# One more step of the main work between a modulation chunk's multiply-adds and its sums over partitions

## The chip, the cores and the metric

The kernel runs on one core of a Trainium2 chip. The metric is the device time of one execution in microseconds (us). Engines are named as the profile names them: PE (TensorE, the matrix engine; PEld is its weight load), DVE (VectorE), ACT (ScalarE), POOL (GpSimd) and SP (SyncE, which only issues DMA transfers here). PSUM is the small memory that PE writes; it is handed out in banks of 128 x 512 floats.

## The reference

Two layers work on x and ctx, each 256 tokens by 1024 (batch 1). Cut to what matters here:

```python
for l in range(2):
    mod_x = silu(c) @ w_mod[l] + b_mod[l]        # six vectors of 1024: shift, scale, gate, twice
    mod_c = silu(c_ctx) @ w_mod[l] + b_mod[l]    # the same weights, for ctx
    hx = rmsnorm(x) * (1 + sc1x) + sh1x;  hc = rmsnorm(ctx) * (1 + sc1c) + sh1c
    mx, mc = token_mixer(hx, hc, ...)             # half Fourier, half gated linear attention; w_in, w_out
    x = x + g1x * mx
    hx = rmsnorm(x) * (1 + sc2x) + sh2x
    x = x + g2x * channel_mixer(hx, l)            # layer 0: a dense FFN; layer 1: 8 experts, 2 per token
    if l == 0:
        ctx = ctx + g1c * mc;  hc = ...;  ctx = ctx + g2c * channel_mixer(hc, l)
return rmsnorm(x) * final_norm_w
```

All arithmetic is f32. A modulation is a matrix-vector product: one vector of 1024 against 1024 x 6144 weights, 24 MB a layer.

## The kernel before

**Main work.** Weights are streamed from HBM in units of 128 x 1024 floats, issued from SP's queue. Each unit is split into a high and a low part (ACT L148, DVE L152), and every product is three matmuls (L159, L160, L161). In time the program goes: mixer 0 (projections by w_in, attention, Fourier part, then w_out, whose results DVE scales and adds at L840 and L841), the FFN of layer 0 (three groups of an up phase, w1 and w3, and a down phase, w2, whose results DVE scales and adds at L1092 and L1093), mixer 1, then the experts. Each switch needs a norm: DVE scales a row block (L958), PE transposes it (L298), and ACT or DVE write the high and low parts of the blocks (low parts on DVE at L313), which are the operand of the next phase. The FFN's first up products take the blocks of ctx alone, half width, and then those of x.

**Modulations.** Of layer 0 the first two vectors are made at the start on PE. All the others, 20 chunks of 512 columns, are made beside the main work by `mod_chunk`, a Python generator. A chunk has four steps. Each loads a unit of w_mod (256 rows, 512 KB) into one of three places of a ring (`rr`, the first two tiles of it) and lets DVE multiply it by the entries of c and add it up in an accumulator of 128 x 512 (L422): one multiply-add for each 128 rows and each vector, so 4 a step where both x and ctx are wanted (`n_src` 2), else 2. Then the accumulator has to be summed over its 128 partitions: for a gate along rows by one matmul with a matrix of ones (L428) and a copy by ACT (L429), for shifts and scales along columns by four small matmuls (L432) and a copy by DVE (L434). The PSUM bank for it (`small`) comes from a ring of four that the main work uses as well.

**Order.** The main work advances the chunks by `pull(mods, 1)` after a step of its own: each pull runs the generator to its next `yield`. So the program's order on every engine is the order in which Python met the steps, but for priorities: the multiply-adds stand under `later(LATER)`, which lets a scheduler put them behind other work by a fixed amount, and splits are given high priority. Mixer 0 has 24 pulls and then takes what is left (`for _ in mods: pass`). It makes six chunks (the gate g of layer 0, 2; shift and scale for the FFN, 4; all for both vectors) and one step of constants. The FFN pulls twice for each of its 22 blocks of 128 and has further pulls in the down phases, 60 in all up to the third group's down phase, ahead of which it takes what is left (`while pull(m1, 1)`). It makes 14 chunks, the last two `gcol`, the second gate of layer 1.

**Gate weights of layer 1.** Behind that drain `gate_weights(1, ...)` loads 32 columns of w_in into the third place of the same ring, lets POOL spread them (L474), and ACT and DVE write their high and low parts (L478, L479) into `wl1`, which lies in the ring's first tile, where chunks load their weights too. Mixer 1 begins with products by `wl1`.

Of the kernel before, what the change touches and what calls it, by code (L numbers as in the profile page):

```python
# [74 lines left out]
def hybrid_kernel(ctx: ExitStack, tc: tile.TileContext, a: dict, out: bass.AP, dbg=None, upto="end"):  # L75
# [19 lines left out]
    def spot(i, n=1):  # L95
        return spots[i // 4][:, i % 4:i % 4 + n, :].rearrange("p a b -> p (a b)")
# [27 lines left out]
    def load_unit(src, shape, ring="raw", queue=None):  # L124
        n = shape[0] * shape[1]
        if ring == "mraw":
            raw = spot(2 * (turn["mraw"] % 3), 2)[:, :n]
            turn["mraw"] += 1
        else:
            raw = place_of("raw", n)  # L130
        ins = (queue or nc.sync).dma_start(raw.rearrange("p (a b) -> p a b", a=shape[0]), src).ins
        if queue:
            return raw, shape
        behind(ins, W.get("load"))
        W["unit"] = ins
        if chained():
            W["load"] = ins
        return raw, shape
# [16 lines left out]
    def wsrc(w2d, r0, nb, c0, cols):  # L155
        return w2d[r0:r0 + nb * 128, c0:c0 + cols].rearrange("(k p) c -> p k c", p=128)
# [83 lines left out]
    def small(shape):  # L240
        return ps0.tile([128, 512], F32, name="sc", tag="sc", bufs=4)
# [164 lines left out]
    def mod_chunk(l, col, n_src, rows_out=None, cols_out=None):  # L406


        accs = []
        for x in range(n_src):  # L410
            acc = spot(10 + x)
            nc.gpsimd.memset(acc, 0.0)
            nc.scalar.dma_start(acc[0:1, :], a["b_mod"][l:l + 1, col:col + 512])
            accs.append(acc)
        for q in range(4):
            raw, _ = load_unit(wsrc(a["w_mod"][l], q * 256, 2, col, 512), (2, 512), ring="mraw")
            rv = raw.rearrange("p (a b) -> p a b", a=2)
            for k in range(2):
                kb = q * 2 + k
                for x in range(n_src):  # L420
                    with later(LATER):
                        nc.vector.scalar_tensor_tensor(accs[x], rv[:, k, :], cs[:, x * 8 + kb:x * 8 + kb + 1],  # L422
                                                       accs[x], op0=OP.mult, op1=OP.add)
            yield
        for x in range(n_src):
            ps = small([128, 512])
            if rows_out is not None:
                nc.tensor.matmul(ps, ones, accs[x], start=True, stop=True)  # L428
                nc.scalar.activation(rows_out[x], ps, AF.Copy)  # L429
            else:  # L430
                for j in range(4):
                    nc.tensor.matmul(ps[:, j:j + 1], accs[x][:, j * 128:(j + 1) * 128], ones[:, 0:1],  # L432
                                     start=True, stop=True)
                nc.vector.tensor_copy(cols_out[x], ps[:, 0:4])  # L434
# [3 lines left out]
    def g_mod(l, which, n_src):  # L438
        col = (2 if which == 1 else 5) * D
        if (l, which) == (1, 2):  # L440

            for hh in range(2):
                yield from mod_chunk(l, col + hh * 512, n_src, cols_out=[gcol[:, hh * 4:(hh + 1) * 4]])
            return
        gp[l, which] = [hbp.tile([128, D], F32, name="g", tag="g1", bufs=1) if l else spot(6 + 2 * x, 2)
                        for x in range(n_src)]
        for hh in range(2):
            yield from mod_chunk(l, col + hh * 512, n_src,
                                 rows_out=[g[:, hh * 512:(hh + 1) * 512] for g in gp[l, which]])

    def s_mod(l, which, n_src):
        mc = modp.tile([128, 2, 16], F32, name="modc", tag="modc", bufs=2)
        modc[l, which] = mc
        for ch in range(4):
            yield from mod_chunk(l, (0 if which == 0 else 3) * D + ch * 512, n_src,
                                 cols_out=[mc[:, x, ch * 4:(ch + 1) * 4] for x in range(n_src)])
# [1410 lines left out]
```

## Time and profile before

| what | value |
|---|---|
| time, median of 3 runs | 1666.74 us (1665.79 to 1666.86) |
| time of the profiled execution | 1666.26 us |
| its span on the core | 1664.4 us |
| mean granted clock of PE | 0.989 of full speed |
| PE busy | 1603.6 us, 96% of the span |
| DVE busy | 1063.1 us, 64% |
| ACT busy | 724.5 us, 44% |
| multiply-adds of the chunks, L422 | 256 rows, 182.0 us |

The span is the stretch that the profiler sees on the core; 1.9 us lie around it. Busy shares are averages over stages that have different limits. The trace of one execution is read in stretches below: mixer 0 lasts to about 255 us, the FFN to 640 us, mixer 1 and the experts fill the rest.

### The profile page before, as it was taken

Reading aid. Unit: us, or ns where it says so; the run is one execution under the profiler, and the core shown is the slowest. Engines: PE = TensorE matmul, PEld = TensorE weight load, DVE = VectorE, ACT = ScalarE, POOL = GpSimd, SP = SyncE. Lnnn points to the kernel's source line nnn. Section 1 sums busy time; section 2 is a strip of 40 time slices with the busy share of each in tenths; the row PEclk is TensorE's granted clock in tenths of the full one; section 3 lists DMA queues with packets and bytes.
Section 4 is the critical chain, followed back from the end, with each engine's and each line's share of the span. In section 5 each row is a group of like instructions: output and inputs, shape, how many; then the busy total and the mean of one; then the engine's idle time right before and its main releaser. Section 6 shows DMA issues by size and latency. Waiting matters only on the chain.

```text
span 1664.4 us, 21388 instructions
## 1 busy us (share of the span) xinstructions
PE 1603.6 (96%) x8014; PEld 1148.3 (69%) x8014; DVE 1063.1 (64%) x1364; ACT 724.5 (44%) x886; POOL 27.5 (2%) x54
## 2 busy tenths in 40 slices
PE   6989999999999999999999989999999999999995
PEld 3867888788888888877787446874367843678431
DVE  3798897788567656865996226872458811688222
ACT  4733455322221247554784125752446710567111
POOL 1000000000000000000000000000000000000000
PEclk9999999999999999999999999999999999999997
DMA  9533385565655534555899999999999999999995
GB/s 372 160 104 126 101 269 154 163 190 169 198 190 191 167 124 134 174 165 215 306 337 322 417 415 414 408 416 417 414 414 413 402 384 415 413 412 411 407 409 202
DMA packets 172441, 479.05 MB, mean 288 GB/s; under 512 B 11777, under 2 KB 65153, under 8 KB 149537
## 3 DMA queue, kind: packets, MB, share of 16 engines
q1 hardware_dynamic: 170896, 473.80, 76.5%
q10 hardware_dynamic: 1074, 2.72, 0.5%
q8 instruction: 67, 1.10, 0.3%
q0 software_dynamic: 352, 1.00, 0.2%
q14 instruction: 52, 0.43, 0.1%
HBM read 476.43 MB, written 1.05 MB: 287 GB/s over the span
## 4 chain that ended last, share of the span: by engine, by line
PE 84%; DVE 6%; DMA 5%; ACT 3%; issue 1%; SPq 0%; POOL 0%; ACTq 0%; DVEq 0%; POOLq 0%
PE h L1647 12%; PE mm L159 8%; PE mm L160 8%; PE mm L161 8%; PE h L1656 6%; PE h L1659 6%; PE h L1655 6%; PE y L159 5%; PE y L160 5%; PE y L161 5%; PE y L1679 4%; DMA raw<-moe_w 3%; PE sc L601 1%; DVE lo L152 1%; PE sc L1624 1%
## 5 line engine op out<-in xcount | busy, mean ns | idle before, releaser
L180 DVE TENSOR_TENSOR rb<-raw,rb 128x2048 fp32r<-128x2048 f32 x72 | 164.8, 2291 | 174.7 <-ACT rb L180 160.3
L148 ACT ACTIVATE hi<-raw 128x1024 fp32r<-128x1024 f32 x127 | 134.5, 1059 | 303.1 <-PE mm L160 88.0
L152 DVE TENSOR_TENSOR lo<-raw,hi 128x1024 fp32r<-128x1024 f32 x127 | 155.2, 1223 | 80.9 <-ACT hi L148 79.5
L180 ACT ACTIVATE rb<-raw 128x2048 fp32r<-128x2048 f32 x72 | 138.1, 1918 | 119.2 <-DMA raw<-moe_w 62.8
L422 DVE SCALAR_TENSOR_TENSOR rr<-rr,cs,rr 128x512 f32<-128x512 f32 x256 | 182.0, 748 | 10.7 <-DMA rr<-b_mod 5.2
L1656 PE MATMUL h<-rb,hg 128*128 128x512 f32 x448 | 177.8, 397 | 4.0 <-DVE rb L180 4.0
L159 PE MATMUL mm<-hbk,hi 128*128 128x512 f32 (+1 forms) x456 | 166.5, 366 | 1.1 <-DVE tm L840 1.0
L160 PE MATMUL mm<-hbk,hi 128*128 128x512 f32 (+1 forms) x456 | 163.7, 360 | 0.5 <-DVE hbk L313 0.5
L161 PE MATMUL mm<-hbk,lo 128*128 128x512 f32 (+1 forms) x456 | 163.8, 359 | 0.0
L1647 PE MATMUL h<-raw,hgs 128*64 128x512 f32 (+1 forms) x608 | 134.3, 539 | 0.0
L1655 PE MATMUL h<-rb,hg 128*128 128x512 f32 x288 | 108.7, 399 | 5.1 <-ACT rb L180 5.1
L1656 PEld LDWEIGHTS h<-rb,hg 128*128 128x128 f32 x448 | 85.3, 190 | 26.9 <-DVE rb L180 6.8
L1647 PE MATMUL h<-rr,hgs 128*64 128x512 f32 (+1 forms) x416 | 98.2, 547 | 0.0
L159 PEld LDWEIGHTS mm<-hbk,hi 128*128 128x128 f32 x456 | 85.9, 189 | 16.6 <-issue 2.7
L160 PEld LDWEIGHTS mm<-hbk,hi 128*128 128x128 f32 x456 | 86.0, 189 | 14.1 <-issue 1.0
L161 PEld LDWEIGHTS mm<-hbk,lo 128*128 128x128 f32 x456 | 86.1, 189 | 13.1
L1647 PEld LDWEIGHTS h<-raw,hgs 128*64 128x64 f32 x608 | 45.5, 137 | 71.6 <-issue 66.6
L180 DVE TENSOR_TENSOR rb<-rr,rb 128x2048 fp32r<-128x2048 f32 x37 | 84.5, 2290 | 14.6 <-issue 8.5
L1659 PE MATMUL h<-rb,hg 128*128 128x512 f32 x288 | 89.0, 395 | 2.5 <-DVE hg L180 2.5
L160 PE MATMUL y<-rb,ht 128*128 128x512 f32 x224 | 88.8, 397 | 0.0
L180 ACT ACTIVATE rb<-rr 128x2048 fp32r<-128x2048 f32 x37 | 71.0, 1918 | 21.9 <-PE y L161 11.5
L1679 PE MATMUL y<-raw,hts 128*64 128x512 f32 x308 | 76.5, 601 | 3.5 <-DMA raw<-moe_w 3.4
(385 smaller groups left out, 2957.1 us busy)
## 6 DMA issues: line engine op xcount, KB each, us to landing
raw<-moe_w SPq DMA_DIRECT2D x180, 1024.0 KB
rr<-moe_w SPq DMA_DIRECT2D x106, 1024.0 KB
rr<-w_mod SPq DMA_DIRECT2D x80, 512.0 KB
raw<-ffn_w SPq DMA_DIRECT2D x72, 512.0 KB
raw<-moe_w SPq DMA_DIRECT2D x30, 768.0 KB
raw<-w_in SPq DMA_DIRECT2D x32, 512.0 KB
rr<-moe_w SPq DMA_DIRECT2D x18, 768.0 KB
raw<-w_out SPq DMA_DIRECT2D x23, 512.0 KB
```

The costliest lines, as they stand in the source:

```text
L148: ins = nc.scalar.activation(hi, raw, AF.Copy).ins
L152: nc.vector.tensor_tensor(lo, raw, hi.bitcast(F32), op=OP.subtract)
L159: nc.tensor.matmul(ps, lh, rh, start=start, stop=False)
L160: nc.tensor.matmul(ps, lh, rl, start=False, stop=False)
L161: nc.tensor.matmul(ps, ll, rh, start=False, stop=stop)
L180: r = getattr(self.engine, name)(*args, **kw)
L422: nc.vector.scalar_tensor_tensor(accs[x], rv[:, k, :], cs[:, x * 8 + kb:x * 8 + kb + 1], accs[x], op0=OP.mult, op1=OP.add)
L1647: nc.tensor.matmul(H[i][b][x * 64:x * 64 + 64, :n], HG[e][:, k0 + j, :], hi[:, j, o:o + n], start=(k0 + j == 0), stop=(k0 + j == 7))
L1655: nc.tensor.matmul(H[i][b], hgh[:, kb, :], hi[:, j, bc], start=(kb == 0), stop=False)
L1656: nc.tensor.matmul(H[i][b], hgh[:, kb, :], lo[:, j, bc], start=False, stop=False)
L1659: nc.tensor.matmul(H[i][b], hgl[:, kb, :], hi[:, j, bc], start=False, stop=(kb == 7))
L1679: nc.tensor.matmul(Y[e][0][hh * 64:hh * 64 + 64], ht[:, j0 + j, half], hi[:, j, xc], start=on, stop=off)
```

## The change

One `yield` is added between the four steps of a chunk and its sums. Nothing else differs; lines behind it move down by one (L428 becomes L429, L432 L433, L434 L435).

```diff
@@ mod_chunk
                         nc.vector.scalar_tensor_tensor(accs[x], rv[:, k, :], ...
                                                        accs[x], op0=OP.mult, op1=OP.add)
             yield
+        yield
         for x in range(n_src):
             ps = small([128, 512])
```

Before, the pull behind a chunk's fourth step made its sums and the next chunk's first step. Now that pull runs to the new `yield` and issues nothing; the sums and the next chunk's first step come one pull later. A chunk takes five pulls and not four: mixer 0's six chunks and one step of constants need 31 pulls and not 25, the FFN's 14 chunks 70 and not 56.

**The second chunk's sums (PE, in the attention of mixer 0).** L601 is the attention's score product, L159 to L161 are the projection by w_in, `rr_66` is the tile of the accumulators, `sqc` holds the ones. Before:

```order
L601 MATMUL sc<-ch_280,km 128x128 x8
L601 MATMUL sc<-ch_281,km 128x128 x8
L159 MATMUL mm<-rb_205,hi 128x512
L160 MATMUL mm<-rb_205,hi 128x512
L161 MATMUL mm<-rb_205,lo 128x512
L159 MATMUL mm<-rb_205,hi 128x512
L428 MATMUL sc<-rr_66,sqc 128x512 x2
L160 MATMUL mm<-rb_205,hi 128x512
```

After, one unit of w_in and a score product further on:

```order
L602 MATMUL sc<-ch_280,km 128x128 x8
L602 MATMUL sc<-ch_281,km 128x128 x8
L159 MATMUL mm<-hi,rb_205 128x512
L160 MATMUL mm<-lo,rb_205 128x512
L429 MATMUL sc<-rr_66,sqc 128x512 x2
L161 MATMUL mm<-hi,rb_205 128x512
```

The sums still stand just behind a score product, but two score products later than before; the first chunk's sums have moved one score product further.

**Between w_out of layer 0 and the FFN (DVE).** L840 and L841 (L841 and L842 after) scale and add the last results of w_out, L958 (L959) scales the two blocks of x for the norm, and L313 writes the low parts of x's blocks, with `h_2427` the first of them. Before:

```order
L264 TENSOR_TENSOR rsy<-rsy,rsv 128x1
L422 SCALAR_TENSOR_TENSOR rr_66<-rr_64,cs,rr_66 128x512
L958 TENSOR_SCALAR xn<-resid_1869,rsy 128x1024
L422 SCALAR_TENSOR_TENSOR rr_66<-rr_64,cs,rr_66 128x512
L422 SCALAR_TENSOR_TENSOR rr_66<-rr_65,cs,rr_66 128x512 x4
L313 TENSOR_TENSOR hbk<-h_2427,hbk 128x256
L313 TENSOR_TENSOR hbk<-h_2431,hbk 128x256
L309 TENSOR_SCALAR h_2440<-y,ac_2327,modc 128x256
L422 SCALAR_TENSOR_TENSOR rr_66<-rr_64,cs,rr_66 128x512
```

After:

```order
L422 SCALAR_TENSOR_TENSOR rr_66<-rr_64,cs,rr_66 128x512
L959 TENSOR_SCALAR xn<-resid_1869,rsy 128x1024
L422 SCALAR_TENSOR_TENSOR rr_66<-rr_64,cs,rr_66 128x512 x3
L422 SCALAR_TENSOR_TENSOR rr_66<-rr_65,cs,rr_66 128x512 x4
L422 SCALAR_TENSOR_TENSOR rr_66<-rr_64,cs,rr_66 128x512 x4
L313 TENSOR_TENSOR hbk<-h_2427,hbk 128x256
L313 TENSOR_TENSOR hbk<-h_2431,hbk 128x256
L309 TENSOR_SCALAR h_2440<-y,ac_2327,modc 128x256
```

From the last L840 pair to `h_2427` there are 10 multiply-adds in the order of before and 16 in that of after. From the last L584 of the attention, which stands about 70 us earlier, to that pair there are 34 and now 48. The 4 that stood among x's low parts have gone ahead of them. The last chunk's column sums (L432, now L433), which stood among w_out's products on PE with ctx's 16 transposes, now stand with the transposes behind the last of these products.

**Between w2 and mixer 1 (PE, then DVE).** L161 on `y` is the last product of w2, `rr_4850` holds the gate weights' parts. On PE, before:

```order
L161 MATMUL y<-hi,rb_4768 128x512
L159 MATMUL mm<-hbk,rr_4850 128x256
L160 MATMUL mm<-hbk,rr_4850 128x256
L161 MATMUL mm<-hbk,rr_4850 128x256
L159 MATMUL mm<-hbk,hi 128x256
```

After:

```order
L161 MATMUL y<-hi,rb_4719 128x512
L433 MATMUL mm<-sqc,rr_66 128x1 x4
L1076 MATMUL mm<-lgb,sqc 128x8
L298 MATMUL mm<-sqc,xn 128x128 x16
L159 MATMUL mm<-hbk,rr_4850 128x256
```

The last sum, the router's small matmul and the 16 transposes of ctx stood among the products of the up phase and of w2. On DVE, after, from the first half of the last results of w2 (L1093 and L1094 are L1092 and L1093 of before):

```order
L1093 TENSOR_TENSOR tm<-y,rr_65 128x512
L152 TENSOR_TENSOR lo<-raw,hi 128x1024
L422 SCALAR_TENSOR_TENSOR rr_66<-rr_65,cs,rr_66 128x512
L1094 TENSOR_TENSOR resid_1867<-resid_1867,tm 128x512
L422 SCALAR_TENSOR_TENSOR rr_66<-rr_64,cs,rr_66 128x512
L1093 TENSOR_TENSOR tm<-y,rr_65 128x512
...
L435 COPY gcol<-mm 128x4
L1077 COPY lgb<-mm 128x8
L263 TENSOR_SCALAR rsv<-rsv 128x1
L959 TENSOR_SCALAR rb_5243<-resid_1867,rsy 128x1024
L480 TENSOR_TENSOR rr_4850<-rr_67,rr_4850 128x512 x2
```

Where "..." stands, three more multiply-adds, one L1094 and six small steps of the norm follow. Before, all multiply-adds and L479 (now L480) stood in the up phase, and the low parts of ctx's blocks (L313) among the L1092 and L1093 of w2; now those low parts follow L480. On SP, the load of the 32 columns of w_in stands behind the last loads of w_mod, and these behind four of the first loads of mixer 1; before, it stood ahead of loads of w2.

## Rows read from the trace of the kernel before

**Rows 1.** The page: busy time of PE; shares of the chain that ended last.

```profile
PE 1603.6 (96%) x8014; PEld 1148.3 (69%) x8014; DVE 1063.1 (64%) x1364; ACT 724.5 (44%) x886; POOL 27.5 (2%) x54
PE 84%; DVE 6%; DMA 5%; ACT 3%; issue 1%; SPq 0%; POOL 0%; ACTq 0%; DVEq 0%; POOLq 0%
```

**Rows 2.** Windows: stretch, length, busy (and count) of each engine, clock, DMA, GB/s.

```profile
300.00:350.00 50.00, 50.00 (x227) 40.98 (x226) 38.08 (x52) 15.39 (x20) 2.10 (x4) 1.00 0.57 176
600.00:650.00 50.00, 49.17 (x258) 41.45 (x257) 36.72 (x68) 30.52 (x59) 0.00 (x0) 1.00 0.50 148
```

**Rows 3.** Waits of PEld, 20 to 640 us: total, times, longest.

```profile
PEld sc L428 <- issue: 4.9, 3, 3.8
PEld sc L428 <- PE mm L161: 1.0, 1, 1.0
```

**Rows 4.** Timeline of PEld at the second sums: start, length, instruction, [idle before].

```profile
120.44 0.19 PEld L159 LDWEIGHTS mm<-rb,hi 128*128 128x128 f32 x1
124.45 0.50 PEld L428 LDWEIGHTS sc<-rr,sqc 128*128 128x128 f32 x2 [3.83 <-issue]
...
127.17 0.32 PEld L160 LDWEIGHTS mm<-rb,hi 128*128 128x128 f32 x1 [0.52 <-issue]
```

**Rows 5.** Timeline of DVE over the same wait.

```profile
119.22 2.18 DVE L422 SCALAR_TENSOR_TENSOR rr<-rr,cs,rr 128x512 f32<-128x512 f32 x3
...
123.66 0.72 DVE L645 COPY_PREDICATED A<-masks,sc 128x512 f32<-128x512 uint8 x1
```

**Rows 6.** Window of 1 us behind that wait, columns as above.

```profile
125.00:126.00 1.00, 1.00 (x2) 0.34 (x1) 1.00 (x3) 0.00 (x0) 0.00 (x0) 0.50 0.85 303
```

**Rows 7.** Timeline of DVE from the attention to x's low parts.

```profile
185.94 8.03 DVE L422 SCALAR_TENSOR_TENSOR rr<-rr,cs,rr 128x512 f32<-128x512 f32 x12
...
264.41 3.40 DVE L422 SCALAR_TENSOR_TENSOR rr<-rr,cs,rr 128x512 f32<-128x512 f32 x5
267.72 0.77 DVE L313 TENSOR_TENSOR hbk<-h,hbk 128x256 fp32r<-128x256 f32 x2
```

**Rows 8.** Windows over that stretch, columns as in group 2.

```profile
186.00:208.00 22.00, 22.00 (x140) 18.00 (x140) 19.54 (x36) 9.42 (x20) 1.33 (x3) 1.00 0.25 73
208.00:255.60 47.60, 47.29 (x228) 38.97 (x226) 43.63 (x76) 26.15 (x47) 2.15 (x4) 1.00 0.80 255
255.60:273.70 18.10, 16.73 (x136) 16.32 (x137) 18.10 (x40) 10.09 (x24) 0.00 (x0) 1.00 0.53 152
```

**Rows 9.** Timeline of PEld, w_out's end and the first up product.

```profile
243.87 1.47 PEld L298 LDWEIGHTS sc<-sqc,xn 128*128 128x128 f32 x12
...
254.77 0.19 PEld L161 LDWEIGHTS mm<-hi,rb 128*128 128x128 f32 x1
256.38 0.19 PEld L159 LDWEIGHTS mm<-hbk,hi 128*128 128x128 f32 x1 [1.43 <-issue]
```

**Rows 10.** Timeline of PEld, the last sum and mixer 1's first product.

```profile
593.08 1.08 PEld L432 LDWEIGHTS mm<-sqc,rr 128*128 128x128 f32 x8
...
640.02 0.19 PEld L159 LDWEIGHTS mm<-hbk,rr 128*128 128x128 f32 x1
```

**Rows 11.** Timeline of DVE: gate weights, then the end of w2.

```profile
583.30 1.29 DVE L479 TENSOR_TENSOR rr<-rr,rr 128x512 fp32r<-128x512 f32 x2
...
640.63 1.28 DVE L1092 TENSOR_TENSOR tm<-y,rr 128x512 f32<-128x512 f32 x2
641.83 1.22 DVE L152 TENSOR_TENSOR lo<-raw,hi 128x1024 fp32r<-128x1024 f32 x1
642.97 1.29 DVE L1093 TENSOR_TENSOR resid<-resid,tm 128x512 f32<-128x512 f32 x2
```

**Rows 12.** Timeline of all engines: load and spreading of the gate weights.

```profile
576.06 0.37 SPq L131 DMA_DIRECT2D rr<-w_in  x1
...
579.88 2.07 POOL L474 COPY rr<-rr 128x128 f32<-128x128 f32 x4 [7.75 <-issue]
```

**Rows 13.** Waits of PEld, 640 to 665 us: total, times, longest.

```profile
PEld sc L298 <- DVE rb L958: 0.9, 1, 0.9
```

## The prediction

> **What bounds the kernel now.** I read the page first: PE is busy for 96% of the span and carries 84% of the chain that ended last [rows 1]. A change that neither adds nor removes PE work can gain only where PE waits and lose only where it makes PE wait. The windows say where that is. In the middle of the FFN PE is busy for 50.00 of 50 us, and DVE for 38.08 [rows 2]: a chunk's multiply-adds and sums have cover there, and moving them changes nothing. That leaves the places where PE idles in mixer 0, and the two joints at which the kernel takes what is left of the chunks at once, because the pulls no longer suffice: the end of mixer 0 and the end of the FFN's last up phase.
>
> **The first two sums.** The waits of PE's weight loads name L428 as the largest single line up to 640 us: 4.9 us in three waits, the longest 3.8, and 1.0 us once behind a product [rows 3]. At the second sums PE stands from 120.6 to 124.45 us [rows 4]. The multiply-adds they need ended at 119.22 + 2.18 = 121.4 us, but PE started only as DVE's first L645 was ending (123.66 + 0.72 = 124.38) [rows 5]. L645 reads the banks of the score product that stands just ahead, and the sums' banks come from the same ring of four. So of the 3.8 us I put some 1 us to the multiply-adds and the rest to the DVE queue and the bank. PE is then slow as well: the window from 125 to 126 us has a granted clock of 0.50 [rows 6], the 1.2 GHz level, and from 124.45 to about 127.8 us PE does 3.4 us of work that the full clock would do in 1.7. The two places thus hold 3.8 + 1.7 + 1.0 = 6.5 us.
>
> After the change the sums stand again a few products behind a score product, two scores later. The multiply-adds are long done by then, the bank is not. If each of the two sums keeps about 1.5 us of waiting for the bank and the clock stays up, 6.5 - 3.0 = 3.5 us are gained. The bounds are 0 (DVE is as late there) and 6.5.
>
> The clock by rows: one idle stretch of 3.83 us, then 0.50. The Trainium skill, page "TensorE: Matmul & The Clock Gate", section "Part 1: The HAM clock gate", says that an idle TensorE falls to its half clock and gets the full one back only with sustained work; the trace agrees here (0.50 behind 3.83 us). By that rule each new long wait of PE at the joints would cost a further 1.7 us (the price that the rows give for this one), and the sum below would be 3.4 us higher with both.
>
> **Joint 1, w_out to the FFN.** Here DVE sets the pace. From 255.6 to 273.7 us it is busy for all of 18.10 us, while PE has 1.4 us to spare [rows 8]; x's first low part starts at 267.72, straight behind five multiply-adds [rows 7], and PE needs it to go from ctx's half-width products to x's. By the order shown with the change, from the attention's last L584 to that low part DVE had 34 + 10 = 44 multiply-adds and has 48 + 16 = 64. Twelve in a row took 8.03 us, so 0.67 each [rows 7], and 20 more are 13.4 us. Against it stands the idle time of DVE in the same stretch: 22 - 19.54 = 2.46 us and 47.6 - 43.63 = 3.97 us [rows 8], 6.4 together, of which I take two thirds, 4.3, since the rest are waits for splits that more multiply-adds do not fill. And the stretch begins earlier by the 3.5 us gained above, which is where that gain is spent. 13.4 - 4.3 - 3.5 = 5.6 us later. The 4 multiply-adds that no longer stand among x's low parts give nothing back, since PE is paced by its own products behind the first block.
>
> PE's own side agrees in sign. The last chunk's column sums and 16 transposes (12 took 1.47 us [rows 9]) stand behind w_out's last product, so the gap of 254.77 to 256.38 us [rows 9] holds 1.1 us for each of two sums and 2.0 of transposes, and the ctx products start later, but they end in front of the same DVE wait. In the FFN behind it PE has no idle time in which to win the loss back [rows 2]. Bounds for the joint: 13.4 - 6.4 - 5 = 2 us (all idle time filled, and the first sums' full gain but for 1.5 us) and 13.4 - 3.5 = 9.9 us (none of it filled).
>
> **Joint 2, w2 to mixer 1.** Now the last product of w2 is followed without a gap by mixer 1's first product at 640.02 us [rows 10], because ctx's norm, its low parts and the gate weights were ready. After the change the last chunk and the gate weights stand behind w2. In the time of before:
>
> w2 ends earlier, since the transposes (2.0 us) and the last column sum (1.08 us [rows 10]) left it: 640.0 - 3.1 = 636.9 us. DVE takes 0.6 us to begin, as now (640.02 to 640.63 [rows 10, 11]), so at 637.5. Then four results at 0.6, one split at 1.14 (641.83 to 642.97 [rows 11]), five multiply-adds at 0.67 and 0.2 for small steps are 7.1 us: the last multiply-add ends at 644.6. PE's sum adds 1.1 us, and two transposes 0.25: 646.
>
> The gate weights take longer. Their load left SP at 576.06 us and POOL began at 579.88 [rows 12], 3.8 us later; from POOL's start to the end of L479 were 583.30 + 1.29 - 579.88 = 4.7 us [rows 11, 12]. In the new order the load is queued behind first loads of mixer 1, which wait for a raw buffer to be split; the last such split now lies between 639 and 641.5 us, so I take 640.5. Then 640.5 + 3.8 + 4.7 = 649.0 us. ctx's low parts stand behind L480 on DVE, so 0.4 us later PE starts: 649.5 us against 640.0, 9.5 us late. L480 cannot start before the last multiply-add either, since it goes into the ring's tile that these still read; that alone would give 644.6 + 1.15 (L478, taken as long as L479) + 1.3 + 0.4, some 647.5 us. During mixer 1's ctx products DVE finishes x's norm, so the 0.9 us that PE waits for it now [rows 13] go, and I add 0.8 us for the clock, half the price above. 9.5 - 0.9 + 0.8 = 9.4 us. Bounds: 647.5 - 640.0 - 0.9 = 6.6, less 1.6 us if some of the multiply-adds run while PE still works on w2, so 5; above, a load that leaves SP 2 us later and the full clock price, 13.
>
> The Trainium skill, same page, section "Architectural detail", says that VectorE's and ScalarE's queues are strictly first in, first out. That rule speaks against this change: L313 cannot pass L480. No run here shows it apart.
>
> **Sum.** Against the profiled execution, 1666.26 us (span 1664.4 and 1.9 around it, 0.5 under the median of the runs): 1666.3 + 5.6 + 9.4 = 1681.3. I say 1681 us.
>
> **The rivals.** Both joints late is the likeliest, 0.60, between 1666.3 + 2 + 5 = 1673 and 1666.3 + 9.9 + 13 = 1689.
>
> Only one joint costs, 0.19. For it speaks that each loss rests on a queue order, and DVE has free time in all stages; against it that DVE has none from 255.6 us on [rows 8] and that joint 2 puts a load, POOL, ACT and DVE in series behind the last product. Joint 1 alone gives 1672, joint 2 alone 1676.
>
> Both cost more, 0.08: both wake at the half clock, and the w_mod loads behind the first w_in loads come late, so that multiply-adds wait for data. That is 1689 and 2 to 5 us, 1692.
>
> Faster, 0.07: the sums' wait was for the multiply-adds after all, so that 6.5 us go; DVE then reaches joint 1 6.5 us early and fills its 6.4 us of idle time, which covers 12.9 of 13.4 us, and at joint 2 the DVE steps and the load run ahead while PE is still on w2. It decides from the point where joint 2 costs under 3 us. That gives 1660 to 1663.
>
> The change does nothing, 0.06: the sums wait for L645's bank as before, and the drained chunks run under other work. 1666.
>
> **How the numbers follow.** What a measurement of this kernel can tell from no change is about 0.2%, or 3.3 us. The forecast is the likeliest case. The range goes from 1671, which takes in either joint alone, to 1690, which takes in the upper bounds; outside lie no change and faster (0.13) and most of the heavy case. Faster 0.07, within 0.2% 0.06, slower 0.87.
>
> **What would show it.** Right: the waits for L429 fall from 5.9 us to about 3, with no window at 0.50 behind them; x's first low part comes some 5 us later than 267.7, behind a run of about 12 multiply-adds; PE has an idle stretch of 8 to 12 us between the last product on `y` and mixer 1's first, in which POOL's L474 and DVE's L480 run. Wrong: mixer 1's first product follows w2 within 3 us, or x's first low part is not later; or the experts' stage, which is not touched, gives back what the joints lost.

## The result, and the profile after

The changed kernel takes 1690.51 us (median of 5 runs, 1689.81 to 1695.15) against 1665.79 us before (median of 5 runs, two more than in the table above): slower by a factor of 1.0156, 95% interval 1.0144 to 1.0168. The factor is taken over all runs; the medians lie 24.7 us apart. The profiled execution has a span of 1688.7 us, 24.3 us more than before.

The page of the changed kernel, busy times and chain:

```profile
PE 1613.7 (96%) x8014; PEld 1158.6 (69%) x8014; DVE 1062.8 (63%) x1364; ACT 726.5 (43%) x886; POOL 27.1 (2%) x54
PE 83%; DMA 6%; DVE 5%; ACT 3%; issue 2%; SPq 1%; DVEq 0%; ACTq 0%
```

The work is the same (8014 matmuls, 1364 DVE instructions, as in [rows 1]). PE is busy 10 us longer, with the same matmuls: some of them ran at half the clock. The rest of the 24 us is idle time of PE. The waits of its weight loads, 20 to 700 us (total, times, longest; "issue" stands where the view names nothing that was waited for):

```profile
PEld mm L433 <- DVE rr L422: 8.6, 2, 8.3
PEld sc L433 <- issue: 5.9, 2, 5.7
PEld sc L429 <- issue: 4.6, 3, 2.5
PEld sc L429 <- PE sc L429: 0.4, 1, 0.4
PEld mm L159 <- ACT h L311: 4.2, 1, 4.2
```

The first row is the last sum of all, at the joint of w2 and mixer 1. The second is the last column sum of mixer 0, at the joint of w_out and the FFN. The third and fourth are the first two sums, 5.0 us together, which waited 5.9 us before [rows 3]. The last is mixer 1's first product.

**First joint.** The timeline of PEld, with the idle time ahead of an instruction in brackets:

```profile
249.63 0.19 PEld L161 LDWEIGHTS mm<-hi,rb 128*128 128x128 f32 x1
255.48 0.28 PEld L433 LDWEIGHTS sc<-sqc,rr 128*128 128x128 f32 x1 [5.66 <-issue]
```

DVE meanwhile, and up to x's first low part:

```profile
255.39 0.74 DVE L422 SCALAR_TENSOR_TENSOR rr<-rr,cs,rr 128x512 f32<-128x512 f32 x1
257.38 0.16 DVE L435 COPY modc<-sc 128x4 f32<-128x4 f32 x1 [1.25 <-PE sc L433]
...
259.09 0.16 DVE L435 COPY modc<-sc 128x4 f32<-128x4 f32 x1 [0.95 <-PE sc L433]
...
271.47 7.38 DVE L422 SCALAR_TENSOR_TENSOR rr<-rr,cs,rr 128x512 f32<-128x512 f32 x11
280.19 0.76 DVE L313 TENSOR_TENSOR hbk<-h,hbk 128x256 fp32r<-128x256 f32 x2 [1.34 <-ACT hbk L312]
```

PE has loaded the last weights of w_out at 249.8 us and soon stands, until DVE is at its last multiply-add of that chunk (255.39 + 0.74 = 256.1; the accumulators of x and ctx are done one after the other). Then DVE stands for PE's sum, and at the end for the block that ACT writes from PE's transposes. x's first low part comes at 280.19, 12.5 us after the 267.72 of [rows 7].

PE was slow in between as well. The transposes of x, which follow ctx's half-width products, began at 278.10 us, 16.0 us after the first of these products; before they began 8.6 us after it. The clock fell a second time there, behind a stretch in which PE was busy for 2.03 of 4 us (windows; columns as in [rows 2], where the engines stand in the order PE, PEld, DVE, ACT, POOL, and the clock is the third figure from the end):

```profile
264.00:268.00 4.00, 2.03 (x12) 1.41 (x11) 3.90 (x12) 3.95 (x11) 0.00 (x0) 0.92 0.01 2
268.00:272.00 4.00, 3.26 (x13) 2.79 (x14) 4.00 (x11) 1.66 (x5) 0.00 (x0) 0.50 0.41 131
```

DVE is busy all the same (3.90 and 4.00 us of 4). So, by the trace, the slow products show in x's first low part only by the 1.34 us that DVE waits at their end.

**Second joint.** PEld:

```profile
648.87 0.19 PEld L161 LDWEIGHTS y<-hi,rb 128*128 128x128 f32 x1
657.33 1.78 PEld L433 LDWEIGHTS mm<-sqc,rr 128*128 128x128 f32 x8 [8.27 <-DVE rr L422]
659.00 0.55 PEld L1076 LDWEIGHTS mm<-lgb,sqc 128*128 128x128 f32 x2
659.28 3.46 PEld L298 LDWEIGHTS mm<-sqc,xn 128*128 128x128 f32 x16
666.94 0.29 PEld L159 LDWEIGHTS mm<-hbk,rr 128*128 128x128 f32 x1 [4.19 <-ACT h L311]
```

The gate weights' last step on DVE, then the low parts of ctx's first two blocks; and on ACT the first and the last steps that read ctx's transposes:

```profile
660.48 1.28 DVE L480 TENSOR_TENSOR rr<-rr,rr 128x512 fp32r<-128x512 f32 x2
...
661.98 0.76 DVE L313 TENSOR_TENSOR hbk<-h,hbk 128x256 fp32r<-128x256 f32 x2
```

```profile
660.62 1.02 ACT L311 ACTIVATE h<-mm,modc,ac 128x256 f32<-128x256 f32 x2 [2.11 <-PE mm L298]
...
665.87 1.02 ACT L311 ACTIVATE h<-mm,modc,ac 128x256 f32<-128x256 f32 x2
```

Mixer 1's first product starts at 666.94 us and not at 640.02 [rows 10], 26.9 us late. The gate weights were ready at 661.76; the product waited 5.2 us longer. Its own block, the first, was ready as well (661.98 + 0.76 = 662.7 for two of them). The product started as ACT's last L311 ended (665.87 + 1.02 = 666.9), and L311 writes no block: it reads the transposes out of their bank of PSUM. So by the trace the product waited for a bank that still held transposes of ctx; no run tries that by itself. ACT's steps begin only when the transposes have come, and the transposes stand behind the sum on PE. Of the 26.9 us the stages behind give back 2.6 (the spans differ by 24.3), nearly all of it the experts' stage, which begins 26.7 us late; what did that was not tried.

The clock behind both idle stretches, in windows:

```profile
258.00:260.00 2.00, 2.00 (x10) 2.00 (x11) 1.05 (x5) 0.00 (x1) 0.52 (x1) 0.50 0.58 217
660.00:662.00 2.00, 2.00 (x11) 2.00 (x10) 1.85 (x5) 1.38 (x4) 0.00 (x0) 0.50 0.00 0
```

### The profile page after: what moved, and what is told of

It is laid out like the page before. It is cut to its first block, busy times and chain, and to the rows that moved or that the text cites. A ratio compares the mean times of both kernels' runs of the same rounds, so it can differ in the third digit from the quotient of the medians.

```text
span 1688.7 us, 21385 instructions
## 1 busy us (share of the span) xinstructions
PE 1613.7 (96%) x8014; PEld 1158.6 (69%) x8014; DVE 1062.8 (63%) x1364; ACT 726.5 (43%) x886; POOL 27.1 (2%) x54
## 4 chain that ended last, share of the span: by engine, by line
PE 83%; DMA 6%; DVE 5%; ACT 3%; issue 2%; SPq 1%; DVEq 0%; ACTq 0%
PE h L1648 11%; PE mm L159 9%; PE mm L160 8%; PE mm L161 8%; PE h L1657 6%; PE h L1660 6%; PE h L1656 6%; PE y L160 5%; PE y L159 5%; PE y L161 5%; PE y L1680 4%; DMA raw<-moe_w 4%; PE sc L602 1%; PE sc L1625 1%; DMA rb<-w_mod 1%
## 5 line engine op out<-in xcount | busy, mean ns | idle before, releaser
L148 ACT ACTIVATE hi<-raw 128x1024 fp32r<-128x1024 f32 x127 | 134.4, 1059 | 309.7 <-PE mm L160 88.2
L152 DVE TENSOR_TENSOR lo<-raw,hi 128x1024 fp32r<-128x1024 f32 x127 | 155.2, 1223 | 86.4 <-ACT hi L148 85.3
L422 DVE SCALAR_TENSOR_TENSOR rr<-rr,cs,rr 128x512 f32<-128x512 f32 x256 | 181.4, 746 | 4.1 <-DMA rr<-b_mod 1.6
L159 PE MATMUL mm<-hbk,hi 128*128 128x512 f32 (+1 forms) x456 | 167.6, 369 | 1.8 <-ACT hbk L312 1.7
L160 PE MATMUL mm<-hbk,hi 128*128 128x512 f32 (+1 forms) x456 | 166.1, 365 | 1.0 <-DVE rsv L263 0.9
L161 PE MATMUL mm<-hbk,lo 128*128 128x512 f32 (+1 forms) x456 | 165.1, 362 | 0.0
L159 PEld LDWEIGHTS mm<-hbk,hi 128*128 128x128 f32 x456 | 87.5, 192 | 17.2 <-ACT hbk L312 2.5
L161 PEld LDWEIGHTS mm<-hbk,lo 128*128 128x128 f32 x456 | 87.8, 193 | 12.9
L180 DVE TENSOR_TENSOR rb<-rr,rb 128x2048 fp32r<-128x2048 f32 x37 | 84.4, 2289 | 14.2 <-issue 9.1
L180 DVE TENSOR_TENSOR rb<-raw,part 128x2048 fp32r<-128x2048 f32 x32 | 73.2, 2289 | 10.6 <-ACT part L180 7.7
```

Source lines behind the costliest of these rows:

```text
L148: ins = nc.scalar.activation(hi, raw, AF.Copy).ins
L152: nc.vector.tensor_tensor(lo, raw, hi.bitcast(F32), op=OP.subtract)
L159: nc.tensor.matmul(ps, lh, rh, start=start, stop=False)
L160: nc.tensor.matmul(ps, lh, rl, start=False, stop=False)
L161: nc.tensor.matmul(ps, ll, rh, start=False, stop=stop)
L180: r = getattr(self.engine, name)(*args, **kw)
```

## The experiments

Two theories stood at first. A: the loss is the chunks that the pulls no longer reach; they are drained at the two joints with PE standing there. B: the step itself costs, in every chunk.

**The step in one of the two places alone.** A flag that `mods0` and `mods1` set, in the changed kernel:

```diff
             yield
-        yield
+        if more[0]:
+            yield
```

In mixer 0 alone:

> The added step stands only in the six chunks of mixer 0. Theory A (the loss is the last chunk that the pulls no longer reach, drained behind w_out and behind w2, with PE standing there): only the first joint costs, 1674 to 1678 us, first full-width product some 10 us late, and the w2 to mixer 1 joint without an idle stretch, as before. Rival B (every chunk loses because its accumulator is held one step longer): six of twenty chunks, 24.7 x 6/20 = 7 us, 1673, spread over mixer 0 and with no idle stretch of 5 us in front of L433. Rival C (the two joints add more together than alone): under 1670.

Measured: 1678.21 us, ratio 1.0069 (1.0051 to 1.0088), 0.2 us above A's range. In the FFN alone:

> The added step stands only in the FFN's 14 chunks. Theory A: only the joint of w2 and mixer 1 costs, 1680 to 1684 us, with PE idle some 8 us in front of L433 and again some 4 us in front of mixer 1's first product. Rival B: 14 of 20 chunks, 24.7 x 14/20 = 17 us, 1683, but lost over the up phases. Rival C: under 1676.

Measured: 1680.98 us, ratio 1.0092 (1.0072 to 1.0111). Against their before (1666.43) the two lose 11.8 and 14.6 us, 26.3 together, where both at once lost 24.7. So the joints add, which disposes of C. B's times lie too near to be told from A's, but the trace of the first run has 5.67 us of idle time in front of the last sum, where B had no stretch of 5.

**The same drains without the step.** The kernel of before with fewer pulls:

```diff
         for _ in tok(U0, tl, sink_u):
             pull(G, 1)
-            pull(mods, 1)
```

> The kernel of before, without the added step; the four pulls in the loop over U of mixer 0 are left out, so that as much of the last chunks is left for the drain as in the changed kernel. Theory A: the drain alone does it, so it costs what the changed kernel lost at the first joint plus the some 3.5 us that the first sums had gained: 1677 to 1682 us. Rival B: sums directly behind their multiply-adds cost nothing, 1665 to 1669.

Measured: 1678.28 us, ratio 1.0078 (1.0056 to 1.01). The other drain:

```diff
-            pull(m1, 2)
+            pull(m1, 2 if f < 10 else 1)
```

> The kernel of before, without the added step; the FFN pulls once and not twice for its blocks 10 to 21, so that the last two chunks are drained as in the changed kernel. Theory A: as with the added step in the FFN alone, 1680 to 1684 us, PE idle some 8 us in front of the last sum. Rival B: 1665 to 1669.

Measured: 1679.71 us, ratio 1.0086 (1.0065 to 1.0107), 0.3 us under A's range. Without any added step both lose what the step loses. PEld in the second of them:

```profile
637.74 0.19 PEld L161 LDWEIGHTS y<-hi,rb 128*128 128x128 f32 x1
646.20 0.93 PEld L432 LDWEIGHTS mm<-sqc,rr 128*128 128x128 f32 x4 [8.27 <-DVE rr L422]
```

It is the wait of the changed kernel, 8.27 us (8.1 in the run with the step in the FFN alone). B falls.

**The step with enough pulls.** If only the drains cost, more pulls should cure it. First in both places, the extra ones of mixer 0 in the loops over V and G:

```diff
             pull(G, 1)
-            pull(mods, 1)
+            pull(mods, 2)
...
-            pull(m1, 2)
+            pull(m1, 3 if f < 10 else 2)
```

> The added step, with pulls added so that none is missing: mixer 0 pulls twice in the loops over V and G (32 for 31), the FFN three times for its first ten blocks (70 for 70). The first sums then stand where they stood before. Theory A (the whole loss is the chunks that the pulls no longer reach): no idle stretch over 2 us at either joint, 1664 to 1668 us, as before. Rival B (the step itself costs): 1672 and above.

Measured: 1676.18 us, ratio 1.0061 (1.0046 to 1.0077). Then with those of mixer 0 in the loop over U and in the Fourier part:

> The added step, with the missing pulls added later in mixer 0 (twice in the loops over U and the Fourier part) and as in the run before in the FFN. The first sums stand where the changed kernel has them. Theory A: the gain at the first two sums (3.7 us earlier at the end of the attention in the changed kernel) stays and nothing is lost: 1661 to 1664 us, if the six chunks' multiply-adds, now crowded into the last third of mixer 0, do not make DVE late at w_out; 1665 to 1669 if they do. Rival B: 1672 and above.

Measured: 1675.72 us, ratio 1.0064 (1.0051 to 1.0078). A missed both, by 8 and by 7 us. The times are where B put them, but the trace doesn't show B's reason. The second joint is cured; in the run with late pulls PE is busy from 600 to 650 us:

```profile
600.00:650.00 50.00, 49.94 (x235) 41.23 (x234) 36.20 (x62) 29.03 (x51) 2.01 (x4) 1.00 0.49 145
```

The first joint is not, though no chunk is left for it. DVE there, in the same run:

```profile
266.99 6.71 DVE L422 SCALAR_TENSOR_TENSOR rr<-rr,cs,rr 128x512 f32<-128x512 f32 x10
273.61 0.76 DVE L313 TENSOR_TENSOR hbk<-h,hbk 128x256 fp32r<-128x256 f32 x2
```

x's first low part is 5.9 us later than in [rows 7], behind ten multiply-adds in a row where five stood. In the run with early pulls it is 8.8 us later. Nor is mixer 0 all of the loss: at mixer 1's first product the runs are 9.4 and 10.8 us late. In both PE waits 1.4 us for ACT's L148 and 0.9 us for DVE's L152 where the FFN first turns to w2 (at 350.25 and 351.93 us in the run with late pulls), which it did not before; the extra pulls stand in the blocks ahead of that turn. To settle the FFN by itself, the step there alone with three pulls from block 10 on:

> The added step in the FFN's 14 chunks alone, with pulls added (three instead of two from the FFN's block 10 on), so that nothing is left for the drain in front of w2's last phase. If the FFN's step costs only by the chunks that it leaves for that drain: as before, 1664 to 1668 us, no idle stretch over 1.5 us between 600 and 650 us. If the step itself costs in the up phases: 1670 and above.

Measured: 1666.46 us, ratio 0.9999 (0.999 to 1.0009). So in the FFN A holds: the 14.6 us come from the drain and, within 0.1%, none from the step, if the pulls stand in the later blocks.

**Mixer 0: who is short there?** Two runs on the kernel of before. One gives the first two sums the later place and pushes no multiply-add back. The sums of these two chunks are kept and made ahead of the next chunk's second load:

```diff
-            acc = spot(10 + x)
+            acc = rows_out[x] if wait else spot(10 + x)
...
+        owed.append(sums)
+        if not wait:
+            pay()
...
+            if q == 1:
+                pay()
             raw, _ = load_unit(wsrc(a["w_mod"][l], q * 256, 2, col, 512), ...
```

> The kernel of before, with the sums of its first two chunks alone made one step later, behind the next chunk's first step, so that no pull is spent and no multiply-add moves back (these two chunks add up in the tiles of their result rows, so that the next chunk does not need their accumulators). Theory A, sharpened: the step costs only by the multiply-adds that it pushes back, and gains at the first two sums, so this has the gain alone: the waits in front of these sums fall from 5.9 us to 2 to 4, no 0.50 window behind them, 1660 to 1664 us. Rival D: DVE is the limit of mixer 0 from the attention on, so that PE gets the 3 us early to the joint and waits there: 1665 to 1667.

Measured: 1666.5 us, ratio 1.0004 (0.9995 to 1.0013): no gain. The time is D's, but not for D's reason: the waits in front of these sums are still 5.6 us, and the clock still falls:

```profile
99.77 0.30 PEld L438 LDWEIGHTS sc<-rr,sqc 128*128 128x128 f32 x2 [2.51 <-issue]
```

```profile
100.00:104.00 4.00, 4.00 (x8) 1.93 (x8) 4.00 (x8) 1.75 (x4) 0.00 (x0) 0.57 0.30 111
```

DVE is busy for all 4.00 us there. The sum starts 0.07 us after DVE's first reading of the score product (98.98 + 0.72 = 99.70 us) has ended, as in [rows 4, 5]. The other run pulls chunks earlier, without the step:

```diff
         for _ in tok(U0, tl, sink_u):
             pull(G, 1)
-            pull(mods, 1)
+            pull(mods, 2)
```

> The kernel of before, without the added step, with two pulls for one in mixer 0's loop over U, so that its last two chunks come four pulls earlier and nothing is left to take at its end. If multiply-adds done before the joint are what counts there, x's first low part comes 2 to 5 us earlier: 1661 to 1664 us. If DVE is full in the Fourier part as well, PE waits there for the low parts of its own operands and it is no gain: 1665 to 1672.

Measured: 1671.86 us, ratio 1.0034 (1.0021 to 1.0047). The time lies in the second range, but PE does not wait for low parts. Now an earlier column sum waits for its multiply-adds (the first of two ends at about 154.5 us):

```profile
154.61 0.52 PEld L432 LDWEIGHTS sc<-sqc,rr 128*128 128x128 f32 x4 [3.18 <-issue]
```

Earlier costs, later costs: in each of the runs that moved pulls of mixer 0, PE stood for DVE somewhere.

**What holds PE at the joints.** In the changed kernel, half of the multiply-adds of the two drained last chunks left out:

```diff
-            for k in range(2):
+            for k in range(1 if half else 2):
```

> The changed kernel with half of the multiply-adds of the two drained last chunks left out (8 of 16 in mixer 0, 4 of 8 of gcol's second half; their results are then not the reference's), all loads, sums and orders left in. If DVE's multiply-adds in front of the drained sums hold PE: 8 x 0.67 = 5.4 us less at the first joint, whose wait in front of L433 all but goes, and 4 x 0.67 = 2.7 us less at the second, 1681 to 1684 us. Rival (the load of the last unit, or the order of the sum and the transposes on PE, holds it): within 2 us of the changed kernel, 1688 to 1691.

Measured: 1681.02 us, ratio 1.0096 (1.008 to 1.0111), 9.5 us less than the changed kernel. The last sum of the first joint waits 0.32 us and not 5.66, and x's first low part comes at 272.17 and not 280.19. That is 8.0 us earlier where the multiply-adds alone are 5.4: the rest is idle time of DVE, 6.1 us from the attention's last L584 to that low part, as before (6.4), and not 8.65. At the second joint:

```profile
646.48 0.71 PEld L433 LDWEIGHTS mm<-sqc,rr 128*128 128x128 f32 x3 [5.22 <-DVE rr L422]
```

5.22 us and not 8.27: less by 3.05, where 4 x 0.67 = 2.7 was worked out. So DVE's multiply-adds hold PE at both joints.

**The order of sum and transposes at the second joint.** The last sum taken out of the drain and made behind w2:

```diff
-            while pull(m1, 1):
-                pass
+            pull(m1, 10)
...
-                    pull(m1, 1)
+                    pull(m1, 0 if last else 1)
```

> The changed kernel with the very last sum (gcol's second half, wanted only behind the experts) left out of the drain and made behind w2, so that it no longer stands in front of ctx's 16 transposes; its multiply-adds and the gate weights stay where they are. Theory Q (PE stands at the sum while the transposes and so ctx's blocks are queued behind it): the transposes go back among w2's products, mixer 1's first product follows L480 and no longer ctx's blocks, 4 to 6 us less: 1684 to 1687 us. Rival (multiply-adds and gate weights alone hold mixer 1): within 1 us of the changed kernel, 1689.5 to 1691.

Measured: 1690.6 us, ratio 1.0155 (1.014 to 1.0171), no different from the changed kernel. Its trace shows why the gain was small and did not last:

```profile
650.55 0.19 PEld L161 LDWEIGHTS y<-hi,rb 128*128 128x128 f32 x1
661.51 1.78 PEld L433 LDWEIGHTS mm<-sqc,rr 128*128 128x128 f32 x8 [10.77 <-issue]
663.69 0.29 PEld L159 LDWEIGHTS mm<-hbk,rr 128*128 128x128 f32 x1 [0.40 <-issue]
```

```profile
659.16 1.45 POOL L475 COPY rr<-rr 128x128 f32<-128x128 f32 x4 [19.82 <-DMA rr<-w_in]
```

```profile
662.03 1.29 DVE L480 TENSOR_TENSOR rr<-rr,rr 128x512 fp32r<-128x512 f32 x2
```

Mixer 1 starts 3.2 us earlier, and no longer waits for the readings of ctx's transposes. The multiply-adds and the gate weights (their load now later, POOL at 659.16) hold it next. The experts begin 2.1 us earlier, and by their end the span is 0.3 us shorter.

**The clock.** Six unread matmuls ahead of the last sum, in the changed kernel:

```diff
+            if q in warm:
+                filler = small([128, 512])
+                for _ in range(6):
+                    nc.tensor.matmul(filler, ident, raw[:, 0:512], start=True, stop=True)
```

> The changed kernel with six extra matmuls of 128 x 512 ahead of the drained last sum, on the last unit of w_mod as it lands (some 3 us behind w2's last product), whose result nobody reads. PE then works in most of the 8 us before that sum. Theory K (the half clock behind the idle stretch is a good part of the loss): sum, transposes and first products of mixer 1 at the full clock, 2 to 4 us less, 1686.5 to 1688.5 us. Rival (the chain of multiply-adds, sum, transposes and blocks on DVE and ACT sets the time, not PE's speed): under 1 us, 1689.5 to 1691.

Measured: 1697.02 us, ratio 1.0194 (1.0178 to 1.021), outside both ranges. As a test of the time it failed: the fillers' data came late and they began at half the clock, so that the sum itself stood behind them. The trace is of the shortest of its four executions, 1692.79 us.

```profile
655.09 0.45 PEld L427 LDWEIGHTS mm<-rr,sqc 128*128 128x128 f32 x2 [4.22 <-DMA rr<-w_mod]
...
661.61 0.19 PEld L437 LDWEIGHTS mm<-sqc,rr 128*128 128x128 f32 x1 [0.24 <-issue]
...
669.29 0.29 PEld L159 LDWEIGHTS mm<-hbk,rr 128*128 128x128 f32 x1 [4.51 <-DVE h L309]
```

But it bounds a price. From the start of the sum to mixer 1's first product it took 669.29 - 661.61 = 7.7 us here, at the full clock, and 666.94 - 657.33 = 9.6 us in the changed kernel, at half. Up to ACT's first L311, where only PE's sum and transposes stand, it was 663.75 - 661.61 = 2.1 us and 660.62 - 657.33 = 3.3 us. Behind it the two runs differ in more than the clock: with the fillers, which take a bank more, the product waits for another reader of the transposes, DVE's L309. The clock's share of this stretch is thus between 1.1 and 1.9 us; the rest is ACT and DVE.

## Why the prediction was wrong

The direction was right and both joints were the right places; the size was not: 24.7 us and not 15.0 (5.6 + 9.4), half a microsecond outside the range.

**The first sums.** The reading of the wait held: in the changed kernel too the second sum starts 0.07 us after DVE's first reading of the score product ended (138.77 and 138.84 us). But the two sums kept 1.7 and 2.5 us of it, and the waits fell from 5.9 to 5.0 us, not to 3. No window at 0.50 was left behind them in this execution (it was not so in each, see the last section). The attention's last L584 did come 3.7 us earlier (3.5 forecast), but that was luck, as most of it has other reasons. Multiply-adds up to there, in windows filtered to L422 (length, busy time and count, then clock, DMA share, GB/s), of before, of the changed kernel, and of the run without the step and without pulls in the loop over U:

```profile
84.00:185.60 101.60, 33.43 (x48) 0.98 0.38 120
```

```profile
84.00:181.90 97.90, 22.05 (x32) 1.00 0.34 103
```

```profile
84.00:181.60 97.60, 22.17 (x32) 1.00 0.34 103
```

The third has the old places of the first sums, and is as early. What both have in common is 16 multiply-adds not yet done, and on PE the column sums of a chunk: in these stretches PE was busy with column sums for 3.69, 2.00 and 1.84 us. So 1.7 to 1.85 us of the gain are a loan, and 11 us of multiply-adds are owed to the joint. The third is no clean comparison for the rest, since its clock happened to stay up behind the wait of 3.83 us that it shares with the kernel before.

**Joint 1: 5.6 us forecast, 12.5 measured.** The 20 multiply-adds and their price held (13.4 us forecast, 14.2 measured). The step that failed is "of which I take two thirds, 4.3", the idle time of DVE to be filled. Over that stretch, before and after (after in two parts):

```profile
185.94:267.72 81.78, 80.55 (x458) 67.80 (x456) 75.35 (x136) 41.84 (x81) 3.48 (x6) 1.00 0.62 193
```

```profile
182.27:256.10 73.83, 68.56 (x357) 56.34 (x356) 68.83 (x111) 30.98 (x52) 3.47 (x6) 0.98 0.69 220
256.10:280.20 24.10, 21.30 (x118) 19.69 (x118) 20.45 (x49) 10.94 (x29) 1.05 (x2) 0.70 0.34 99
```

DVE was idle for 81.78 - 75.35 = 6.4 us before and for 5.0 + 3.65 = 8.65 us after. Nothing was filled; 2.2 us were added. Its busy time grew by 13.9, so the stretch grew by 16.15 us, less 3.7 for the earlier start: 12.45. The added idle time is the sum that the drain put between the two engines: PE stood for DVE's last multiply-add, then DVE for PE's sum at half the clock (1.25 and 0.95 us), and at the end for the blocks that hang on PE's transposes. With half of the drained multiply-adds the sum hardly waits, and the idle time is back at 6.1 us; even so hardly any of it is filled. The bound "none of it filled", 9.9 us, was no bound, since a new wait in both directions can lengthen idle time. Nor do the ctx products "end in front of the same DVE wait": the multiply-adds ended 1.34 us before ACT's block came.

**Joint 2: 9.4 us forecast, 26.9 - 12.5 = 14.4 measured.** Counted from the end of w2, the chain came as worked out: last multiply-add 8.2 us later (7.7 forecast), gate weights ready 12.7 us later (12.1). The step that failed is "so 0.4 us later PE starts". It started 5.2 us later, as ACT's last reading of ctx's transposes ended. With the transposes behind the sum on PE, as the order showed, all their readings by ACT and DVE come behind it as well, and the product has to wait for a bank of them; I had priced two transposes and one low part, and no bank. With the transposes back among w2's products the first product followed w2's end by 663.69 - 650.78 = 12.9 us, which is the 12.6 forecast for that chain. Two slips in the working are small: 649.0 + 0.4 is 649.4, and the upper bound of 13 leaves out the 0.9 us that the forecast takes off; with it the bound is 12.3.

**The rivals.** The heavy case (1692 us) was nearest: the half clock at both joints did come, but no multiply-add waited for data there. "Faster" rested on the first sums, whose waits fell by 0.9 us and not by 6.5. "Only one joint" was wrong, and so was "nothing".

**The clock.** The granted clock was 0.50 behind 5.66 us of idle time and behind 8.27 us. That agrees with the Trainium skill, page "TensorE: Matmul & The Clock Gate", section "Part 1: The HAM clock gate": an idle TensorE falls to half its clock. It fell a second time at each joint: 0.50 from 268 to 272 us, behind the half-idle stretch shown above, and from 668 to 670 us, behind the 4.19 us. The forecast had 0.8 us for the clock at the second joint and nothing at the first; PE was busy 10 us longer in all. The 1.7 us for each long wait that the rows of before gave lies within the 1.1 to 1.9 us of the second joint, though it is the price of one execution; for the first joint, and for the second falls, it was not measured apart.

**Open.** How the 12.5 us of the first joint divide between order and clock; whether the bank alone holds mixer 1's first product; and what in the stages behind gave back 2.6 us. No version here beat the kernel before.

## What to carry to other kernels

When side work is advanced by pulls from the main work, count the pulls against the steps: one more step for each chunk leaves whole chunks for the place where the rest is taken at once, and that place has no cover. Adding pulls cured it where DVE had time to spare (the FFN's later blocks, 0.9999). It did not in mixer 0, where DVE is busy for 75.35 of 81.78 us from the attention to x's low parts: pulls moved earlier cost time even without the step (1.0034), and with step and extra pulls the times were 1.0061 and 1.0064, part of that lost in the FFN. And when a sum is drained between two engines that wait for each other, price everything queued behind it on both, to the last reading of the bank that the next product needs. Idle time ahead of such a place is not stock to be filled: here hardly any of the 6.4 us was.

## What the runs showed of the hardware

The idle matmuls cost more than they saved: begun 4.22 us after PE's last work they ran at half the clock, the first ones 0.85 us apart (656.06, 656.91, 657.77) and the later ones, once the clock was back, 0.43. A filler whose data came after the clock had fallen delayed what it should help.

The clock did not follow a wait of one length alike in every execution. Behind 3.83 us of idle time at the second sums it was 0.50 from 125 to 126 us in the kernel before, and 1.00 from 124 to 130 us in the run without the step and without pulls in the loop over U. Behind 2.49 us it stayed at 1.00 in the changed kernel and was 0.71 from 140 to 144 us in the run with the step in mixer 0 alone. A price read from one trace is the price of that execution.
